# Decay exponents from one 104-row TensorE product per direction, and modulation from unsplit weights in four column strips

## Chip, cores and metric

The kernel runs on one core of one Trainium2 chip. The metric is the device time of one execution in microseconds (us). Before the change, three runs took 2903.76, 2908.97 and 2911.34 us; the median is 2908.97 us.

## What is computed

Two layers of a hybrid diffusion block over 1024 latent tokens and 256 context tokens, width 1024. Each layer modulates a normalised input, projects it, runs attention, a bidirectional state-space scan (SSD) and retention side by side, and projects the mixture back. Two pieces of the reference matter here. The modulation:

```python
shift, scale, gate = jnp.split(jax.nn.silu(c) @ w_ada + b_ada, 3, axis=-1)
shift_c, scale_c, gate_c = jnp.split(jax.nn.silu(c_ctx) @ w_ada + b_ada, 3, axis=-1)
```

and the inner product of the scan, for each direction with its own step sizes (`vc` is `xs * dt`, `cum` the running sum of `dt * -exp(a_log)` in a chunk of 128 tokens):

```python
decay = jnp.exp(jnp.where(lower, cum[:, :, :, None] - cum[:, :, None], -jnp.inf))
scores = jnp.einsum('bcign,bcjgn->bcijg', qc, kc)
y = jnp.einsum('bcijg,bcijgh,bcjghp->bcighp', scores, decay, vc) + ...
```

## The kernel before

Tokens lie in ten tiles of 128. Dense projections run in three TensorE products of high and low parts (`mm3`, L303 with the weights stationary, L305 with the activations stationary): every weight is loaded raw from HBM, rounded into `wh` by ScalarE (L275) and its remainder put into `wl` by GpSimd, or VectorE for some (L277).

A generator of dense work (`dense_all`) is pulled in slices by the scan, attention and retention phases: `SHARE` sets how many microseconds of dense TensorE work each phase may pull, so that the dense products fill TensorE while the other engines do the element work. The framework's scheduler then orders the instructions of each engine from a simulated timeline; on the chip every engine runs its own list in that order. All DMAs are issued from SP's queue, also in order.

*Modulation* (`ada`): `w_ada` is cut into 24 pieces of 256 columns, each 1 MB. Eight (`ADA0`) are needed before the first projection; sixteen (`late`) are spread over layer 0's attention. A piece is split like other weights, then 16 products (L234) with a 4-column stationary operand (high and low parts of two vectors) give a 4 x 256 row, which two small products with `pick` turn into columns (L240).

*The scan* (`pair_phase`) goes over eight pairs of heads; a pair takes five blocks of 256 tokens in layer 0 and four in layer 1, 72 in all. `dt_chunk` makes the step sizes `dt`, the running sums `ncum` and their rows, stored in DRAM (`cumd`, `cume`). For a block, `load_R` fetches a 512 KB broadcast of the rows of `cumd` one block ahead. `pair_stage1` then makes the 128 x 512 matrix `mt` of two heads and two tiles: per head and tile, ScalarE adds the column of `ncum` to the forward row (L740) and scales the forward scores `gf` by `dt` (L743); VectorE adds the backward scores (L746) and takes the minimum with the backward exponent (L749); one exponential (L751) and one product (L752) end it. `pair_stage2`, one block later (`LAG`), multiplies `mt` with the values (L768) and adds the state terms (L775 to L787). PSUM has two buffers `ps_t` (`pst`), which before the change only transposes and small sums use.

```python
te[:, hh, c, :] = R[:, 0, hh, c, :] + ncum            # L740, ScalarE
mt[:, hh, c, :] = gf * dt_f                           # L743, ScalarE
mt = gb * dt_b + mt                                   # L746, VectorE
te = min(R[:, 1, hh, c, :] + ncum_b, te)              # L749, VectorE
te = exp(te); mt = mt * te                            # L751, L752
```

## Time and profile before

| | |
|---|---|
| profiled execution, its own time | 2905.51 us |
| its span | 2903.7 us |
| median of three runs | 2908.97 us |
| TensorE (PE) busy | 2666.6 us, 92% |
| TensorE weight loads (PEld) busy | 2352.1 us, 81% |
| VectorE (DVE) busy | 1925.0 us, 66% |
| ScalarE (ACT) busy | 1211.0 us, 42% |
| GpSimd (POOL) busy | 890.7 us, 31% |
| mean granted TensorE clock | 0.955 |

The busy share of an engine is a mean over stages. TensorE's ends are modelled, so its busy time is no measure of peak; what counts is how long it is idle, and which wait ended last. The granted clock is 1 at 2.4 GHz and 0.5 at 1.2 GHz; a value between says how a stretch is shared by the two.

### The profile page before, as it was taken

How to read it: one execution, taken by the hardware profiler on the slowest of the kernel's cores; microseconds unless marked ns; L12 is line 12 of the kernel's file. 1: busy time of each engine (PE TensorE's matmuls, PEld its weight loads, DVE VectorE, ACT ScalarE, POOL GpSimd, SP SyncE). 2: the span in 40 equal slices, each digit the busy share in tenths (PEclk: the TensorE clock that was granted, in tenths of full speed). 3: DMA queues.
4: the chain of work that ended last, by engine and by line, in shares of the span. 5: the costliest groups of instructions: out<-in, count | busy, mean ns of one | idle time of the engine just before them, and what ended most of it. 6: DMA issues, size and time to landing. Idle time of an engine off the chain costs nothing. (4 is left out here: it accounts for less than half of the span.)

```text
span 2903.7 us, 46416 instructions
## 1 busy us (share of the span) xinstructions
PE 2666.6 (92%) x17164; PEld 2352.1 (81%) x17164; DVE 1925.0 (66%) x4648; ACT 1211.0 (42%) x3226; POOL 890.7 (31%) x766
## 2 busy tenths in 40 slices
PE   6888998899999989998999988997999999999999
PEld 4676877788888789987878767876888888889887
DVE  7668768766677775647446568778667767564751
ACT  5345445435455544423133344444335444442330
POOL 4532322242343421334241323232331112112540
PEclk8898999899999999999999989998999999999999
DMA  7033334321121211114453033333210000101461
GB/s 241 4 110 106 97 93 119 111 66 41 48 69 47 78 29 41 32 53 147 140 183 100 20 91 95 87 106 105 74 41 19 23 15 23 30 24 51 146 212 55
DMA packets 149362, 230.40 MB, mean 79 GB/s; under 512 B 14480, under 2 KB 74128, under 8 KB 149136
## 3 DMA queue, kind: packets, MB, share of 16 engines
q1 hardware_dynamic: 149136, 227.45, 25.3%
q8 instruction: 135, 2.21, 0.3%
q14 instruction: 91, 0.75, 0.1%
HBM read 191.34 MB, written 36.04 MB: 78 GB/s over the span
## 5 line engine op out<-in xcount | busy, mean ns | idle before, releaser
L303 PE MATMUL mm<-ah,wh 128*128 128x512 f32 (+1 forms) x1680 | 635.2, 378 | 34.8 <-DVE zu L357 8.6
L277 POOL TENSOR_TENSOR wl<-raw,wh 128x512 fp32r<-128x512 f32 x288 | 384.3, 1354 | 827.9 <-ACT wh L275 796.0
L303 PE MATMUL mm<-al,wh 128*128 128x512 f32 (+1 forms) x1680 | 626.0, 373 | 1.0 <-DVE al L277 1.0
L303 PE MATMUL mm<-ah,wl 128*128 128x512 f32 (+1 forms) x1680 | 625.9, 373 | 0.0
L305 PE MATMUL mm<-wh,ah 128*128 128x256 f32 x1568 | 456.6, 291 | 9.8 <-DVE zu L357 3.9
L305 PE MATMUL mm<-wl,ah 128*128 128x256 f32 x1568 | 451.2, 288 | 0.4 <-POOL wl L277 0.3
L305 PE MATMUL mm<-wh,al 128*128 128x256 f32 x1568 | 450.0, 287 | 0.0
L303 PEld LDWEIGHTS mm<-ah,wh 128*128 128x128 f32 x1680 | 324.3, 193 | 91.3 <-issue 12.0
L303 PEld LDWEIGHTS mm<-ah,wl 128*128 128x128 f32 x1680 | 324.0, 193 | 51.9 <-issue 1.4
L303 PEld LDWEIGHTS mm<-al,wh 128*128 128x128 f32 x1680 | 324.8, 193 | 50.3 <-DVE al L277 1.4
L950 ACT ACTIVATE e<-s,nb 128x512 f32<-128x512 f32 (+1 forms) x384 | 231.8, 613 | 203.4 <-DVE nb L945 202.5
L305 PEld LDWEIGHTS mm<-wh,ah 128*128 128x128 f32 x1568 | 303.3, 193 | 15.5 <-DVE zu L357 4.2
L305 PEld LDWEIGHTS mm<-wl,ah 128*128 128x128 f32 x1568 | 303.4, 193 | 3.7 <-POOL wl L277 1.0
L305 PEld LDWEIGHTS mm<-wh,al 128*128 128x128 f32 x1568 | 303.1, 193 | 2.7 <-issue 0.5
L940 DVE TENSOR_REDUCE mx<-s 128x1 f32<-128x512 f32 (+1 forms) x400 | 224.0, 588 | 67.0 <-PE s L938 65.7
L275 ACT ACTIVATE wh<-raw 128x512 fp32r<-128x512 f32 x288 | 169.5, 626 | 203.0 <-PE mm L303 81.0
L938 PE MATMUL s<-kT,qT 128*128 128x512 f32 (+1 forms) x800 | 218.0, 376 | 10.9 <-ACT e L950 9.4
L989 PE MATMUL o<-v,aT 128*128 128x128 f32 x1312 | 175.3, 277 | 0.3 <-DVE aT L118 0.3
L706 POOL TENSOR_TENSOR xw<-xn,dtpk 128x512 f32<-128x512 f32 (+2 forms) x96 | 83.2, 877 | 280.7 <-ACT xn L116 63.4
L989 PEld LDWEIGHTS o<-v,aT 128*128 128x128 f32 x1312 | 164.2, 193 | 3.1 <-DVE aT L118 0.5
L938 PEld LDWEIGHTS s<-kT,qT 128*128 128x128 f32 x800 | 134.7, 195 | 31.4 <-ACT e L950 17.7
L749 DVE SCALAR_TENSOR_TENSOR te<-R,dtpk,te 128x128 f32<-128x128 f32 x288 | 131.4, 495 | 13.4 <-ACT te L740 13.3
(266 smaller groups left out, 4837.3 us busy)
## 6 DMA issues: line engine op xcount, KB each, us to landing
raw<-in_wi_dram SPq DMA_DIRECT2D x176, 256.0 KB
R<-cumd SPq DMA_DIRECT2D x72, 512.0 KB
E<-cume SPq DMA_DIRECT2D x144, 128.0 KB
raw<-in_wa_dram SPq DMA_DIRECT2D x64, 256.0 KB
mr<-mix SPq DMA_DIRECT2D x64, 256.0 KB
wr<-in_wa_dram SPq DMA_DIRECT2D x32, 256.0 KB
raw<-in_wo_dram SPq DMA_DIRECT2D x32, 256.0 KB
x<-xr SPq DMA_DIRECT2D x24, 256.0 KB
```

What stands on the lines that cost most here:

```text
L275: nc.scalar.activation(out=hi, in_=x, func=AF.Copy)
L277: e.tensor_tensor(out=lo, in0=x, in1=hi.bitcast(F32), op=ALU.subtract)
L303: nc.tensor.matmul(ps, lhsT=w, rhs=x, start=st, stop=sp)
L305: nc.tensor.matmul(ps, lhsT=x, rhs=w, start=st, stop=sp)
L706: nc.gpsimd.tensor_tensor(out=xw, in0=xn[:, a:a + m].rearrange("p t (h e) -> p t h e", h=2), in1=self.wend[:, a:a + m, h0:h0 + 2].unsqueez ...
L749: nc.vector.scalar_tensor_tensor(out=te[:, hh, c, :], in0=Rv[:, 1, hh, c, :], scalar=col(self.ncum, c, 1, hh), in1=te[:, hh, c, :], op0=AL ...
L938: nc.tensor.matmul(ps[:, 0:n], lhsT=qT[:, 2 * m + s, :], rhs=kT[m][:, t0:t0 + n], start=(s == 0), stop=(s == 1))
L940: nc.vector.tensor_reduce(out=mx[:, ci:ci + 1], in_=ps[:, 0:n], axis=AX.X, op=ALU.max, negate=len(chunks) == 1)
L950: nc.scalar.activation(out=em[:, t0:t0 + n], in_=pss[ci][:, 0:n], func=AF.Exp, bias=nb, accum_out=z[:, 3 * m + ci:3 * m + ci + 1])
L989: nc.tensor.matmul(po[:, 0:P], lhsT=aT[j], rhs=v[:, j, :], start=(j == b0), stop=(j == NT - 1))
```

## The change

Modulation: `w_ada` is read unsplit as six pieces of 512 columns per layer, straight into the `wh` and `wl` buffers. The stationary operand is plain float32, 32 columns wide (two vectors and zeros). Eight products write four column strips of one PSUM bank; `pick`, now 128 x 2, sums the strips.

Scan: `dt_chunk` also forms ln(dt) (a logarithm, and one Newton step through an exponential), adds it to the negated running sum, and stores high and low parts of both rows in DRAM (`crow`). `decay_bufs` fills two buffers with the constant rows of a 104-row product: a mask of -1e30 in 64 rows, ones and selectors. `load_R` then fetches only the rows that vary, in two small DMAs. For each direction one product gives the whole exponent in PSUM, ScalarE takes the exponential in place, and VectorE multiplies with the scores.

```diff
-            for k in range(KT):
-                for j in range(2):
-                    nc.tensor.matmul(ps[0:4, 0:256], lhsT=self.sc[:, k, :], rhs=w[j][:, k, :],
-                                     start=(k == 0 and j == 0), stop=(k == KT - 1 and j == 1))
+            for j in range(2):
+                for g in range(4):
+                    nc.tensor.matmul(ps[32 * g:32 * g + 32, :], lhsT=self.sc[:, 4 * j + g, :], rhs=w[j][:, g, :],
+                                     start=(j == 0), stop=(j == 1))
...
+    def load_a(self, src, j):
+        t = self.w_p.tile([P, 4, 512], F32, tag=("wh", "wl")[j], name=self.nm("wa"))
+        for g in range(0, 4, 2):
+            self.nc.sync.dma_start(out=t[:, g:g + 2, :], in_=src[:, 4 * j + g:4 * j + g + 2, :])
+        return t
...
+        nc.vector.tensor_scalar(out=z, in0=x, scalar1=1e-37, scalar2=None, op0=ALU.max)
+        nc.scalar.activation(out=u, in_=z, func=AF.Ln)
+        nc.scalar.activation(out=z2, in_=u, func=AF.Exp, scale=-1.0)
...
+        r1, r2 = (self.work(x_, (64, 512), F32R) for x_ in ("r1", "r2"))
+        nc.scalar.activation(out=r1[:, 0:tn], in_=pt[0:64, 0:tn], func=AF.Copy)
+        nc.vector.tensor_tensor(out=r2[:, 0:tn], in0=pt[0:64, 0:tn], in1=r1[:, 0:tn], op=ALU.subtract)
...
     def pair_stage1(self, p, bi, last, R):
...
-        for hh, c in hc:
-            nc.scalar.activation(out=te[:, hh, c, :], in_=Rv[:, 0, hh, c, :], func=AF.Identity,
-                                 bias=col(self.ncum, c, 0, hh))
...
-        nc.scalar.activation(out=te, in_=te, func=AF.Exp)
-        nc.vector.tensor_tensor(out=mt, in0=mt, in1=te, op=ALU.mult)
+        for d, G in enumerate(self.grp[p // 4][2]):
+            ps = self.pst()
+            nc.tensor.matmul(ps, lhsT=lt[0:104, d], rhs=rt[0:104, d], start=True, stop=True)
+            nc.scalar.activation(out=ps, in_=ps, func=AF.Exp)
+            f = ps.rearrange("p (h c i) -> p h c i", h=2, c=2)
+            nc.vector.scalar_tensor_tensor(out=f if d else mt, in0=f, scalar=3e38,
+                                           in1=G[:, c0:c0 + 2, :].unsqueeze(1).to_broadcast([P, 2, 2, P]),
+                                           op0=ALU.min, op1=ALU.mult)
+        nc.vector.tensor_tensor(out=mt, in0=mt, in1=f, op=ALU.add)
...
     def load_R(self, p, bi):
-        R = self.unit("R", (P, 2, 2, 256))
...
+        lt, rt = self.lr[0]
+        self.lr.reverse()
+        src = self.crow[bi].rearrange("(a d p) k h t -> a p k d (h t)", a=2, d=2)
+        self.nc.sync.dma_start(out=rt[64:66].bitcast(F32), in_=src[0, p])
+        self.nc.sync.dma_start(out=lt[96:104].bitcast(F32),
+                               in_=self.crow[bi].rearrange("(a d p) k h (c t) -> a p (k h c) d t", a=2, d=2, c=2)[1, p])
```

The scheduler writes each engine's list anew. Three places in these lists follow.

VectorE, one block of the scan (pair 0) before: `te` and `mt` are the block's two tiles, `R` the broadcast rows; the other rows are states, gates and values of other steps.

```order
L749 SCALAR_TENSOR_TENSOR te_1794<-R_1702,dtpk_654,te_1794 128x128 x4
L722 SCALAR_TENSOR_TENSOR st_1727<-st_1727,dtpk_654,s_1730 128x64 x2
L357 SCALAR_TENSOR_TENSOR zu_1764<-zu_1764,mm_1765 128x256
L746 SCALAR_TENSOR_TENSOR mt_1795<-gb_1613,dtpk_654,mt_1795 128x128
L779 SCALAR_TENSOR_TENSOR cv_648<-cv_648,cols_114,o_1851 128x256
L746 SCALAR_TENSOR_TENSOR mt_1795<-gb_1613,dtpk_654,mt_1795 128x128 x3
L357 SCALAR_TENSOR_TENSOR zu_1764<-zu_1764,mm_1904 128x512
L752 TENSOR_TENSOR mt_1795<-mt_1795,te_1794 128x512
```

The same engine and step after the change; `t` is a PSUM buffer of `ps_t`.

```order
L826 SCALAR_TENSOR_TENSOR cv_411<-cv_411,cols_113,o_1549 128x256
L796 SCALAR_TENSOR_TENSOR mt_1512<-t_1513,gf_1430 128x512
L796 SCALAR_TENSOR_TENSOR t_1517<-t_1517,gb_1431 128x512
L799 TENSOR_TENSOR mt_1512<-mt_1512,t_1517 128x512
L796 SCALAR_TENSOR_TENSOR mt_1592<-t_1593,gf_1430 128x512
```

Nine instructions of a block have become three, all with a PSUM operand.

TensorE in the scan of a later pair before: dense rows (L303) around the value product (L768) and the state product (L775).

```order
L303 MATMUL mm_2611<-al_804,wh_2064 128x512
L775 MATMUL s_2455<-cv_647,sf_2241 128x128 x2
L775 MATMUL s_2455<-cv_647,st_1727 128x128 x2
L303 MATMUL mm_2611<-ah_803,wl_2065 128x512
L768 MATMUL o_2411<-mt_2322,xn_1685 64x128 x4
L303 MATMUL mm_2611<-ah_803,wh_2064 128x512
```

After the change, in such a pair (L310 is the dense product, L815 the value product, L822 the state product, L793 the new product, `lr` its operand buffer):

```order
L793 MATMUL t_1887<-lr_1408 128x512
L310 MATMUL mm_2145<-ah_221,wl_1205 128x512
L310 MATMUL mm_2145<-ah_221,wh_1204 128x512
L310 MATMUL mm_2145<-al_222,wh_1204 128x512
L310 MATMUL mm_2145<-ah_221,wl_1205 128x512
L793 MATMUL t_1967<-lr_1428 128x512
L772 MATMUL s_1898<-xw_1896,bn_1286 128x128 x2
L772 MATMUL s_1906<-xw_1904,bn_1286 128x128 x4
L822 MATMUL s_1920<-cv_410,sf_1630 128x128
L822 MATMUL s_1920<-cv_410,st_1525 128x128
L793 MATMUL t_1971<-lr_1428 128x512
L815 MATMUL o_2013<-mt_1882,xn_1493 64x128 x4
```

Products that feed the exponential now stand in TensorE's list, two for a block, and the next block's can stand a few rows behind.

ScalarE in `dt_chunk` after the change (L621 and L622 are the new logarithm and exponential, L485 evacuates a dense product):

```order
L485 ACTIVATE cv_411<-mm_902,cols_113 128x512
L621 ACT_TABLE_LOAD
L621 ACTIVATE dtw_766<-dtw_766 128x128
L485 ACTIVATE cv_412<-mm_967,cols_113 128x512
L622 ACT_TABLE_LOAD
L622 ACTIVATE dtw_766<-dtw_766 128x128
```

Twelve such table loads have been added, two for each of six chunks.

## Rows read from the trace of the kernel before

**Rows 1.** Stages: length; busy PE, PEld, DVE, ACT, POOL; granted clock, DMA share, GB/s.

```profile
180.00:600.00 420.00, 369.78 (x2307) 317.11 (x2308) 330.07 (x933) 202.85 (x527) 127.35 (x95) 0.92 0.35 107
600.00:1500.00 900.00, 847.13 (x5896) 769.47 (x5896) 584.43 (x1290) 380.91 (x1078) 308.55 (x251) 0.97 0.25 75
1650.00:2090.00 440.00, 386.30 (x2312) 331.65 (x2311) 329.69 (x889) 192.74 (x486) 132.97 (x110) 0.92 0.31 93
```

**Rows 2.** Stretches of 10 us in the scan of both layers, columns as above.

```profile
410.00:420.00 10.00, 5.58 (x33) 4.65 (x32) 5.58 (x21) 6.50 (x17) 4.47 (x3) 0.98 0.26 92
...
500.00:510.00 10.00, 5.73 (x43) 4.29 (x41) 9.93 (x31) 4.76 (x13) 1.42 (x1) 0.92 0.63 184
510.00:520.00 10.00, 3.97 (x18) 2.46 (x18) 9.64 (x17) 5.47 (x13) 5.79 (x2) 0.50 0.26 94
...
2000.00:2010.00 10.00, 5.18 (x24) 3.83 (x24) 10.00 (x16) 5.26 (x13) 6.56 (x4) 0.50 0.34 102
```

**Rows 3.** TensorE's waits, from 176 to 600 us, then 1650 to 2090 us: total, times, longest.

```profile
PE t L149 <- DVE cv L505: 19.3, 5, 5.0
...
PE s L712 <- POOL xw L706: 14.8, 5, 4.6
```

**Rows 4.** Groups of instructions by line: busy us, mean ns, idle before and its releaser.

```profile
L749 DVE SCALAR_TENSOR_TENSOR te<-R,dtpk,te 128x128 f32<-128x128 f32 x288 | 131.4, 495 | 13.4 <-ACT te L740 13.3
...
L746 DVE SCALAR_TENSOR_TENSOR mt<-gb,dtpk,mt 128x128 f32<-128x128 f32 x288 | 112.2, 434 | 0.0
...
L740 ACT ACTIVATE te<-R,dtpk 128x128 f32<-128x128 f32 x288 | 91.8, 391 | 61.1 <-DVE cv L505 21.8 <-DMA R<-cumd 16.0 <-PE o L768 13.5
L743 ACT ACTIVATE mt<-gf,dtpk 128x128 f32<-128x128 f32 x288 | 91.4, 390 | 12.5 <-DVE gf L663 5.1 <-DVE cv L505 3.0 <-PE s L775 2.1
...
L752 DVE TENSOR_TENSOR mt<-mt,te 128x512 f32<-128x512 f32 x72 | 56.8, 789 | 1.4 <-ACT te L751 0.7
...
L751 ACT ACTIVATE te<-te 128x512 f32<-128x512 f32 x72 | 45.0, 625 | 43.6 <-DVE te L749 43.4
```

**Rows 5.** Groups with shapes apart: VectorE and ScalarE on 128 x 512 in PSUM.

```profile
L950 ACT ACTIVATE e<-s,nb 128x512 f32<-128x512 f32 x256 | 173.4, 683 | 203.4 <-DVE nb L945 202.5 <-DVE ri L125 0.5
...
L782 DVE TENSOR_TENSOR s<-s,E 128x512 f32<-128x512 f32 x64 | 44.3, 692 | 3.6 <-DMA E<-cume 3.1 <-PE s L775 0.3
```

**Rows 6.** Timeline of the scan: start, length, engine, line; dense products at full clock.

```profile
253.11 0.40 PE L303 MATMUL mm<-ah,wl 128*128 128x512 f32 x1
...
253.34 0.39 PE L303 MATMUL mm<-ah,wh 128*128 128x512 f32 x1
```

**Rows 7.** The start: one 5 us stretch (columns of rows 1), then timeline rows.

```profile
15.00:20.00 5.00, 5.00 (x36) 3.24 (x35) 4.50 (x5) 3.85 (x7) 4.84 (x4) 1.00 0.99 342
...
40.00:45.00 5.00, 3.48 (x21) 1.82 (x19) 4.74 (x14) 1.47 (x6) 3.32 (x2) 0.84 0.59 208
...
12.12 0.38 PE L234 MATMUL mm<-wh,sc 128*4 128x256 f32 x1 [12.12 <-ACT wh L275]
...
52.59 0.69 PE L534 MATMUL mm<-ah,wdt 128*64 128x512 f32 x1
...
59.78 0.50 PE L303 MATMUL mm<-ah,wh 128*128 128x512 f32 x1
```

**Rows 8.** Timeline: modulation products 0.11 us apart, then float32 products, two records each.

```profile
20.10 0.28 PE L234 MATMUL mm<-wl,sc 128*4 128x256 f32 x1
...
20.21 0.28 PE L234 MATMUL mm<-wh,sc 128*4 128x256 f32 x1
...
254.93 1.38 PE L712 MATMUL s<-xw,bn 128*128 128x128 f32 x10
...
267.67 0.66 PE L768 MATMUL o<-mt,xn 128*64 128x128 f32 x8
```

**Rows 9.** The one table load of ScalarE, durations in ns.

```profile
L214 ACT ACT_TABLE_LOAD  x1: 1283/1283/1283, 0.7 to 0.7; - x1
```

**Rows 10.** Weight loads of TensorE that waited for nothing shown: total, times, longest.

```profile
PEld o L768 <- issue: 22.5, 25, 4.4
```

More of the change, by code (lines that the diff above doesn't have):

```diff
@@ L624, in dt_chunk @@
         nc.scalar.activation(out=flat(self.wend), in_=flat(self.wend), func=AF.Exp)
         yield
-        nc.vector.tensor_tensor(out=flat(self.wend), in0=flat(self.wend), in1=flat(self.dt), op=ALU.mult)
+        nc.vector.tensor_tensor(out=flat(self.wend), in0=flat(self.wend), in1=x, op=ALU.mult)
         pt = self.pst()
         for j in range(m):
-            nc.tensor.transpose(pt[0:32, j * P:(j + 1) * P], self.ncum[:, i0 + j, :], self.ident)
-        for nm, func, store in (("cumd", AF.Copy, self.cumd), ("cume", AF.Exp, self.cume)):
-            row = self.work(nm, (32, 512))
-            nc.scalar.activation(out=row[:, 0:tn], in_=pt[0:32, 0:tn], func=func, scale=-1.0)
-            store[c] = self.d_p.tile([8, 2, 2, tn], F32, tag=f"{nm}{l}{c}", name=f"{nm}{l}{c}")
+            nc.tensor.transpose(pt[0:64, j * P:(j + 1) * P], nn[:, j].rearrange("p a h -> p (a h)"), self.ident)
@@ new lines, in dt_chunk @@
+        r1, r2 = (self.work(x_, (64, 512), F32R) for x_ in ("r1", "r2"))
+        nc.scalar.activation(out=r1[:, 0:tn], in_=pt[0:64, 0:tn], func=AF.Copy)
+        nc.vector.tensor_tensor(out=r2[:, 0:tn], in0=pt[0:64, 0:tn], in1=r1[:, 0:tn], op=ALU.subtract)
+        row = self.work("cume", (32, 512))
+        nc.scalar.activation(out=row[:, 0:tn], in_=pt[0:32, 0:tn], func=AF.Exp, scale=-1.0)
+        self.cume[c] = self.d_p.tile([8, 2, 2, tn], F32, tag=f"cume{l}{c}", name=f"cume{l}{c}")
+        for d in range(2):
+            nc.sync.dma_start(out=self.cume[c][:, d], in_=row[16 * d:16 * d + 16, 0:tn])
@@ new lines, in dt_chunk, with decay_bufs @@
+        for b in range(tn // 256):
+            st = self.d_p.tile([32, 2, 2, 256], F32, tag=f"crow{l}{c}{b}", name=f"crow{l}{c}{b}")
+            self.crow[2 * c + b] = st
+            for k, r in enumerate((r1, r2)):
+                nc.sync.dma_start(out=st[:, k], in_=r[:, 256 * b:256 * b + 256].bitcast(F32))
+        yield
+    def decay_bufs(self):
+        nc = self.nc
+        self.lr = []
+        for k in range(2):
+            t = self.unit("lr", (P, TOK), F32R)
+            rt = t[:, 0:1024].rearrange("p (d n) -> p d n", d=2)
+            lt = t[:, 1024:1280].rearrange("p (d n) -> p d n", d=2)
+            self.lr.append((lt, rt))
+            if k:
+                nc.gpsimd.tensor_copy(out=t[0:104], in_=t0[0:104])
+                return
+            t0 = t
+            id64 = self.ident[0:64, 0:64]
+            w = self.work("lrw", (P, 4, 64))
+            nc.vector.memset(t.bitcast(F32)[64:P], 0.0)
+            for d, m in enumerate((self.uf, self.ub)):
+                nc.vector.tensor_tensor(out=w[0:64, d], in0=m[0:64, 0:64], in1=id64, op=ALU.subtract)
+                nc.scalar.activation(out=lt[0:64, d].rearrange("p (q r) -> p q r", r=2),
+                                     in_=w[0:64, d].unsqueeze(2).to_broadcast([64, 64, 2]), func=AF.Copy, scale=-1e30)
+                nc.scalar.activation(out=lt[64:66, d], in_=self.ones[64:66].to_broadcast([2, P]), func=AF.Copy,
+                                     scale=-1.0)
+                for q in range(4):
+                    nc.scalar.activation(out=rt[0:64, d, q * P:(q + 1) * P].rearrange("p (q r) -> p q r", r=2),
+                                         in_=id64.unsqueeze(2).to_broadcast([64, 64, 2]), func=AF.Copy)
+            nc.vector.tensor_tensor(out=w[96:104, 2, 0:4], in0=self.ident[96:104, 96:100],
+                                    in1=self.ident[96:104, 100:104], op=ALU.add)
@@ L1262, in w_order @@
         wi, wa = self.a["wi"], self.a["wa"]
-        q = [(wa[0, i], "gv") for i in ADA0] if l == 0 else []
-        late = iter([(wa[0, i],) for i in range(8, 12)] + [(wa[1, i],) for i in range(12)])
+        q = [(wa[0, i], "ada") for i in ADA0] if l == 0 else []
+        late = iter([(wa[0, i], "ada") for i in (4, 5)] + [(wa[1, i], "ada") for i in range(6)])
         for i in range(N_W):
@@ L1289, in dense_all @@
             yield from xz(5 + j, 3 + j)
-        late = iter([(0, n) for n in range(8, 12)] + [(1, n) for n in range(12)] if l == 0 else [])
+        late = iter([(0, n) for n in (4, 5)] + [(1, n) for n in range(6)] if l == 0 else [])
         def more(i):
@@ L1344, in layer @@
         self.phase(chain(self.dt_rest, self.bc_prep(0, last), self.pair_prep(0),
-                         self.g_prep(0, last)), 26)
+                         self.decay_bufs(), self.g_prep(0, last)), 26)
         share = SHARE[l]
@@ L1393, in run @@
             if j % 2:
-                next(h0)
-                next(h0)
-            if j == 4:
+                for _ in range(4):
+                    next(h0)
+            if j == 2:
                 self.load_dt(0)
```

87 lines of the change are left out of this document (39 added, 48 removed).

## The prediction

> **What bounds the kernel now.** I read the shares of the page first: TensorE is busy for 92% of the span, so at most some 237 us of idle time can be won, and every instruction added to TensorE costs its length wherever TensorE has no gap. Next the busy time by stage, to find the gaps. [rows 1] The two scan stages, 420 and 440 us long, have TensorE busy for 369.8 and 386.3 us: together 50.2 + 53.7 = 104 us of idle time. Their granted clock is 0.92. With 1 for the 2.4 GHz level and 0.5 for the 1.2 GHz level, (1 - 0.92) / 0.5 = 16% of 860 us, 138 us, ran at the low level. The attention stage between them (600 to 1500 us) is 94% busy at 0.97: there TensorE's work is the path.
>
> Then smaller stretches inside a scan, to see who is busy while TensorE is not. [rows 2] At 500 to 520 and 2000 to 2010 us TensorE works for 4.0 to 5.7 of 10 us while VectorE works for 9.6 to 10.0. The first row, at 410 us, is the counterexample: TensorE 5.6 and VectorE also 5.6, a gap at the border of two pairs that no faster VectorE fills. The waits of TensorE say the same. [rows 3] Its longest wait in layer 0 is for a product of VectorE (L505), not of the block itself but queued behind block work; layer 1 has 14.8 us behind GpSimd. So in the scan VectorE is the queue that ends last most often, and TensorE is the engine that pays.
>
> **The change, part by part.** Sums stand against the profiled execution, 2905.5 us; the median of the runs is 3.5 us higher.
>
> *VectorE and ScalarE of a block.* Removed from VectorE are the three groups of 131.4, 112.2 and 56.8 us: 300.4 us, or 4.17 us for each of 72 blocks. [rows 4] Added are three operations on 128 x 512 with a PSUM operand. The nearest row takes 692 ns [rows 5], so 2.08 us a block. VectorE loses 2.09 x 72 = 151 us of the 660 us that it works in the two scan stages, and falls from 77% to 59% of them. ScalarE loses 91.8 + 91.4 + 45.0 = 228 us and gets 144 exponentials in PSUM; by the 683 ns of the one with an accumulator [rows 5] that is 98 us. None of this counts by itself, because neither engine sets the end; it counts through TensorE's gaps.
>
> *TensorE's gaps in the scan.* Of 104 us idle I take 58 us back. Most gaps are of the kind in the last three of rows 2, VectorE saturated; the ones like the first stay. The ends are 20 us (about the 19.3 us that the first of rows 3 shows behind VectorE) and 88 us (85%). With fewer gaps the clock falls less often. Of the 138 us at the low level I take half as matmul time, since the low rows show TensorE 40 to 52% busy [rows 2]; at the full level 69 us become 35, so 35 us is the upper end. I take 25, with 5 as the lower end.
>
> *New products on TensorE.* Two products with 512 columns for each block. Dense products of that width start 0.23 us apart [rows 6], so 144 x 0.23 = 33 us, all on TensorE's list, and all path once the gaps close. A product with 104 rows for 128 takes the same columns; I see no row for less.
>
> Net in the scan: -58 - 25 + 33 = **-50 us**, ends -100 and +8 (-20 - 5 + 33).
>
> *Before the first block.* Twelve table loads of 1.28 us [rows 9] are 15 us of ScalarE. In the four chunks of six that are not a layer's last, dense products cover them, though the evacuations of their PSUM stand behind the loads on ScalarE. The last chunk of a layer gets two loads, a logarithm, an exponential, three VectorE operations and a trip through DRAM before the first block, and `decay_bufs` its fills on ScalarE and one on GpSimd. I take +3 us a layer, **+6 us**; the ends are 0 (the dense work of that phase covers all) and +16 (all table loads exposed).
>
> *Late modulation, layer 0's attention.* Before, a piece of 256 columns is 16 products 0.11 us apart [rows 8], 1.8 us; sixteen pieces are 29 us. After, a piece of 512 columns is 8 float32 products. A float32 product is two records in this trace: the value product stands four times in a row of the list and is eight records [rows 8]. So there are 16 passes of 512 columns. What does a pass take? The eight records of L768 span 0.66 us, one of them 0.27 long, so they start 0.056 us apart at 128 columns; that makes 0.22 us at 512 and 3.6 us a piece if strips run one after another. The full-width records of L712 start (1.38 - 0.28) / 9 = 0.12 us apart, four times that is 0.49 us, 7.8 us a piece: the bad end. If four strips run side by side a piece takes 0.9 us: the good end. I take 2.2 us, between the two that the strip rows allow: 8 x 2.2 = 18 us, **-11 us**; ends -22 and +33. The small `pick` products stay: eight records for a piece twice as wide. The rounding of these weights by ScalarE and GpSimd goes; both are off the path there, so it counts nothing.
>
> TensorE: Matmul & The Clock Gate (Part 3: Packing small matmuls) in the Trainium skill says that small products in different column strips run at once, and gives 2.38x for three strips. By that figure, as an estimate, a piece would take some 1.5 us and this term would be -17 us. The rows of before cannot show it, because no two strips there have a wide moving operand.
>
> *The start.* Layer 0's first four pieces (8 MB) are still loaded, but no split stands between load and product. Before, the first modulation product starts at 12.1, the first projection product at 52.6 and the first dense one at 59.8 us; DMA carries 342 GB/s early and 208 GB/s at 40 us. [rows 7] At 342 GB/s, 8 MB and the 2 MB of `x` take 31 us. Pieces now use the two `wh` and `wl` buffers, so the third waits until the first is multiplied, and the norm still stands after the last. I take **-12 us**, ends -20 and -4.
>
> *Queues.* SP issues two small DMAs where it issued one of 512 KB. Each waits for a product two blocks back to give up its buffer, and behind it stand `E` and raw weights; a block lasts 420 / 40 = 10.5 us, so one block ahead covers it. I cost it at nothing. If that cover is gone, TensorE itself waits at L793, with the dense rows behind it, where before only ScalarE waited (16.0 us on `R` [rows 4]).
>
> Sum: -50 + 6 - 11 - 12 = -67 us: 2838.5 us against the profiled execution, and **2842 us** for the median.
>
> **Rivals.**
>
> *VectorE was the whole cause.* All block gaps close: the scan gives -100 us, and the sum is -117: 2792 us. For it: saturated rows 2. Against: the row at 410 us and GpSimd's 14.8 us. Chance 0.18.
>
> *The strips cost more.* The late pieces take the bad end, +33 instead of -11: 2842 + 44 = 2886 us. For it: weight loads of the 64-column strip product waited 22.5 us in 25 waits that nothing explains [rows 10], 0.9 us each; a piece enters and leaves strips too. TensorEngine Tiling (Key Properties) in the Trainium skill says that changing the tiling mode drains TensorE, which would be such a wait. Against: eight pieces enter and leave only 16 times, 14 us at that price. Chance 0.10.
>
> *The relief does not reach TensorE.* Gaps at pair borders, chains and GpSimd stay; 20 us of gaps and clock come back together while the new products cost 33. The scan is +13 and the sum -4 us: 2905 us, no difference. For it: rows 3 name operations outside the block. Chance 0.09.
>
> *Two PSUM buffers stop TensorE* (slower). A block now holds each `ps_t` buffer from the product over the exponential to VectorE's read, and the next block's product, or a transpose, stands a few rows behind in TensorE's list. If ScalarE or VectorE is late, all dense rows behind wait. The bare chain is 0.23 + 0.68 + 0.69 = 1.6 us, about what stands between two such products in the list. It decides from (67 + 9) / 72 = 1.1 us of added wait a block; at 1.5 us it is 108 us: 2950 us. Against: VectorE at 59% has fewer backlogs of the 5 us kind. Chance 0.11.
>
> **How the numbers follow.** My forecast, 2842 us, has 0.52; its own range is 2805 to 2880. About 0.3%, 9 us, can be told from no change, so faster means below 2900 and slower above 2918. Faster takes the forecast, the first and the second rival: 0.52 + 0.18 + 0.10 = 0.80. The same is 0.09, slower 0.11. The range runs from 2780 (just under the first rival) to 2910 (over the third), and leaves out the slower case and the far good end of the scan and the strips, some 0.18.
>
> **What would show it.** VectorE busy in all near 1925 - 151 = 1774 us, ScalarE down by some 130 us less new fills; L793 at 144 records, 0.23 us apart from the next; TensorE idle in the two scans near 104 - 58 = 46 us with a clock near 0.96; L234 at 192 records, and a late piece in 2 to 3 us; the first dense product near 47 us. Wrong would be: L793 waiting on VectorE or on the DMA of `lr` by more than 1 us a block; idle time in the scans over 80 us; a late piece over 4 us; table loads inside the blocks.

## The result, and the profile after

The changed kernel took 2870.82 us (median of four runs, 2866.96 to 2876.57) against 2906.36 us for the kernel before: a ratio of 0.9878, 95% interval 0.9854 to 0.9902. It is faster by 1.2%, 35.5 us, inside the range and about half of the 67 us forecast. The profiled execution took 2869.1 us, its span is 2867.3 us, 36.4 us less than before, with a mean granted clock of 0.964 for 0.955. All ratios in this document leave out one execution of e8 that took 8641.68 us.

The busy time of the changed kernel, from the page:

```profile
PE 2665.5 (93%) x17116; PEld 2339.0 (82%) x17116; DVE 1781.3 (62%) x4213; ACT 1056.4 (37%) x2678; POOL 772.1 (27%) x688
```

TensorE (PE) is as busy as before within 1.1 us, so all that was won was idle time. VectorE lost 144 us and ScalarE 155 us; neither shows in the time as such. To see where the 36.4 us went I cut both spans at the same events of the program, because the stages moved. Dense products slide over the border between a scan and the step to the first score, and between attention and retention, so those are added up:

| stretch, us | before | after | difference | forecast |
|---|---|---|---|---|
| to the first dense product | 59.8 | 42.0 | -17.8 | -12 |
| to the first value product, layer 0 | 130.9 | 146.0 | +15.1 | +3 |
| scan and step to the first score, layer 0 | 464.9 | 447.2 | -17.7 | -50 for both layers |
| attention, retention, end of layer 0 | 942.6 | 928.1 | -14.5 | -11 |
| layer 1 to its first value product | 116.9 | 121.1 | +4.2 | +3 |
| scan and step to the first score, layer 1 | 419.5 | 400.2 | -19.3 | (above) |
| attention and retention, layer 1 | 649.8 | 663.4 | +13.6 | 0 |
| tail | 119.3 | 119.3 | 0 | 0 |

The busy time by stretch, first the kernel before: the scans of layers 0 and 1, then layer 1's attention and retention. The columns are the stretch, its length, busy time (and instructions) of PE, weight loads, DVE, ACT and POOL, granted clock, DMA share, GB/s.

```profile
190.70:611.10 420.40, 374.97 (x2352) 322.73 (x2353) 330.47 (x917) 199.41 (x518) 132.87 (x98) 0.92 0.36 107
1715.10:2086.60 371.50, 325.57 (x1983) 280.64 (x1982) 287.73 (x780) 165.54 (x423) 113.76 (x91) 0.92 0.33 101
2134.60:2784.40 649.80, 617.91 (x4255) 563.22 (x4254) 434.83 (x1014) 279.24 (x824) 162.38 (x141) 0.98 0.15 47
```

The same three of the changed kernel:

```profile
188.00:576.80 388.80, 373.67 (x2361) 318.41 (x2361) 262.72 (x673) 124.59 (x234) 113.93 (x88) 0.95 0.21 66
1684.40:2036.20 351.80, 335.56 (x2041) 285.96 (x2041) 234.57 (x597) 110.77 (x210) 110.70 (x90) 0.94 0.20 59
2084.60:2748.00 663.40, 620.13 (x4255) 564.25 (x4254) 440.33 (x1014) 279.19 (x824) 160.77 (x141) 0.98 0.15 46
```

Length less busy time is TensorE's idle time: 45.4 + 45.9 = 91 us in the scans before, 15.1 + 16.2 = 31 us after, 60 us back where 58 were forecast. The last row is the surprise: layer 1's attention and retention have the same number of instructions on TensorE, 4255, and take 13.6 us more, 11.4 of them idle, though no line of that code was changed.

What answers to [rows 4] and [rows 5], the operations of a block in the changed kernel. First its groups by line: busy time, mean ns, idle time in front.

```profile
L794 ACT ACTIVATE t<-t 128x512 f32<-128x512 f32 x144 | 82.2, 582 | 146.5 <-PE t L793 142.5 <-DVE v L118 1.4 <-DVE cv L826 1.2
L796 DVE SCALAR_TENSOR_TENSOR t<-t,gb 128x512 f32<-128x512 f32 x72 | 49.9, 694 | 7.6 <-ACT t L794 7.5
L796 DVE SCALAR_TENSOR_TENSOR mt<-t,gf 128x512 f32<-128x512 f32 x72 | 49.5, 687 | 54.8 <-ACT t L794 53.1 <-PE s L772 1.3 <-PE o L815 0.3
L799 DVE TENSOR_TENSOR mt<-mt,t 128x512 f32<-128x512 f32 x72 | 49.2, 683 | 0.4
```

Three operations of 0.68 to 0.69 us, as taken from the 692 ns of [rows 5]; the exponential takes 0.58 us for the 0.68 taken. The new product, with two of the waits in front of it or of its weight load (us, times):

```profile
L793 PE MATMUL t<-lr x144: 389/475/796, 183.8 to 2029.0; 104*128 104x512 f32 x144
...
  DVE mt L796: 19.2, 17
...
  DMA lr<-crow: 3.0, 2
```

All waits of that view add up to some 35 us over 72 blocks, half a microsecond each, where the slower rival decides from 1.1 us; in front of the products themselves 13.6 us are left, 7.4 of them for `mt`. The two small transfers cost 3 us.

### The profile page after: what moved, and what is told of

Same layout as the page of the kernel before. It is cut to its first block, busy times and chain, and to the rows that moved or that the text cites. A ratio compares the mean times of both kernels' runs of the same rounds, so it can differ in the third digit from the quotient of the medians.

```text
span 2867.3 us, 45100 instructions
## 1 busy us (share of the span) xinstructions
PE 2665.5 (93%) x17116; PEld 2339.0 (82%) x17116; DVE 1781.3 (62%) x4213; ACT 1056.4 (37%) x2678; POOL 772.1 (27%) x688
## 4 chain that ended last, share of the span: by engine, by line
PE 76%; DVE 12%; ACT 3%; issue 2%; DMA 2%; POOL 1%; SPq 0%; DVEq 0%; ACTq 0%; POOLq 0%
PE mm L310 34%; PE mm L312 18%; PE t L149 5%; PE o L1037 4%; PE s L986 4%; PE s L772 2%; PE s L822 2%; DVE mx L988 2%; PE o L815 2%; PE t L793 1%; ACT e L998 1%; DVE e L1016 1%; DMA mr<-mix 1%; DVE rs L1156 1%; PE s L1146 1%
## 5 line engine op out<-in xcount | busy, mean ns | idle before, releaser
L310 PE MATMUL mm<-ah,wh 128*128 128x512 f32 (+1 forms) x1680 | 629.4, 375 | 30.1 <-DVE xr L1223 13.8
L310 PE MATMUL mm<-al,wh 128*128 128x512 f32 (+1 forms) x1680 | 622.8, 371 | 1.5 <-DVE al L284 0.9
L310 PE MATMUL mm<-ah,wl 128*128 128x512 f32 (+1 forms) x1680 | 622.4, 371 | 0.6 <-POOL wl L284 0.6
L284 POOL TENSOR_TENSOR wl<-raw,wh 128x512 fp32r<-128x512 f32 x224 | 294.5, 1335 | 769.5 <-ACT wh L282 736.9
L310 PEld LDWEIGHTS mm<-ah,wh 128*128 128x128 f32 x1680 | 322.3, 192 | 85.8 <-issue 13.8
L310 PEld LDWEIGHTS mm<-al,wh 128*128 128x128 f32 x1680 | 322.2, 192 | 51.1 <-issue 1.4
L310 PEld LDWEIGHTS mm<-ah,wl 128*128 128x128 f32 x1680 | 321.2, 191 | 51.2 <-POOL wl L284 1.1
L282 ACT ACTIVATE wh<-raw 128x512 fp32r<-128x512 f32 x224 | 130.0, 625 | 226.2 <-PE mm L310 103.9
L986 PEld LDWEIGHTS s<-kT,qT 128*128 128x128 f32 x800 | 134.3, 193 | 41.3 <-ACT e L998 26.5
L794 ACT ACTIVATE t<-t 128x512 f32<-128x512 f32 x144 | 82.2, 582 | 146.5 <-PE t L793 142.5
```

Source lines behind the costliest of these rows:

```text
L282: nc.scalar.activation(out=hi, in_=x, func=AF.Copy)
L284: e.tensor_tensor(out=lo, in0=x, in1=hi.bitcast(F32), op=ALU.subtract)
L310: nc.tensor.matmul(ps, lhsT=w, rhs=x, start=st, stop=sp)
L794: nc.scalar.activation(out=ps, in_=ps, func=AF.Exp)
L986: nc.tensor.matmul(ps[:, 0:n], lhsT=qT[:, 2 * m + s, :], rhs=kT[m][:, t0:t0 + n], start=(s == 0), stop=(s == 1))
```

## The experiments

Twelve kernels ran. Ratios are against the kernel before, timed on the same chip; the changed kernel itself has 0.9878, and 0.001 is 2.9 us.

| run | ratio | 95% interval |
|---|---|---|
| e1, decay part alone | 0.9930 | 0.9916 to 0.9944 |
| e2, modulation part alone | 0.9892 | 0.9874 to 0.9911 |
| e3, no logarithm on ScalarE | 0.9891 | 0.9874 to 0.9908 |
| e4, one column strip | 0.9972 | 0.9963 to 0.9982 |
| e5, dt steps in twos | 0.9855 | 0.9841 to 0.9870 |
| e6, VectorE work put back | 0.9886 | 0.9870 to 0.9902 |
| e7, products twice | 0.9916 | 0.9898 to 0.9933 |
| e8, three PSUM buffers | 0.9932 | 0.9909 to 0.9954 |
| e9, e5 and another list | 0.9821 | 0.9805 to 0.9837 |
| e10, block in small pieces | 0.9991 | 0.9981 to 1.0000 |
| e11, transfers put back | 0.9924 | 0.9903 to 0.9944 |
| e12, kernel before, another list | 1.0027 | 1.0016 to 1.0039 |

The ratio is of the whole time, and each new list also moves layer 1's attention, which no run here edits (last section of the experiments). So the scans are given by themselves too, from the profiled executions, in us: scans and steps to the first score of both layers, TensorE's idle time in the two scans, and layer 1's attention and retention.

| kernel | scans and steps | idle in the scans | attention and retention, layer 1 |
|---|---|---|---|
| before | 884.4 | 91 | 649.8 |
| changed | 847.4 | 31 | 663.4 |
| e1 | 853.9 | 39 | 648.3 |
| e2 | 880.8 | 81 | 650.0 |
| e6 | 857.5 | 42 | 649.0 |
| e7 | 863.7 | 30 | 651.3 |
| e8 | 873.9 | 50 | 659.3 |
| e10 | 894.6 | 46 | 644.1 |
| e11 | 870.9 | 48 | 646.7 |

e1, e3, e4, e5 and e9 have the scan's code of the changed kernel, and 845.9 to 853.9 us there; so differences up to 7 us say nothing.

### Which part brought the time (e1, e2)

e1 is the kernel before with the new `dt_chunk`, `decay_bufs`, `pair_stage1` and `load_R`; e2 is the rest of the diff. Against the changed kernel:

```diff
 e1
-ADA0 = (0, 2, 1, 3)
+ADA0 = (0, 4, 1, 5, 2, 6, 3, 7)
...
 e2
-            nc.tensor.matmul(ps, lhsT=lt[0:104, d], rhs=rt[0:104, d], start=True, stop=True)
-            nc.scalar.activation(out=ps, in_=ps, func=AF.Exp)
...
+            nc.scalar.activation(out=te[:, hh, c, :], in_=Rv[:, 0, hh, c, :], func=AF.Identity,
+                                 bias=col(self.ncum, c, 0, hh))
...
```

> The decay part alone (new exponent product, exp in PSUM, new dt chain), with the modulation of the kernel before. Theory A (the prelude's own chains of norm and dt swallow an early start, and the decay part earns only in the scans): the two scans together 45 to 55 us shorter than before with TensorE idle there down from 91 to 30 to 40 us, the prelude 4 to 10 us longer, the time 2862 to 2875. Theory B (the new dt steps are what spoils the prelude, +15 us or more there): time 2875 to 2890, and the modulation part alone then keeps its start. Rival C (VectorE was not what held the scans, the gain came with the other part): time above 2895.

> The modulation part alone (unsplit weights in four strips, LATE, first four pieces), with the decay blocks and dt steps of the kernel before. Theory A: first dense product at about 42 us, but chunk 1 stalls as before and the first value product comes at about 183 to 191 us all the same; late pieces earn about 9 us; time 2888 to 2900. Theory B: the first value product at 170 to 176 us, so the head start of 18 us is kept; time 2872 to 2884. If the +10 us of layer 1's attention in the changed kernel comes from this part, attention there is 484 to 488 us here too, else 475 to 478.

Measured, for the stretches of the table above. e1: -0.1, +10.2, -17.0, +3.7, +4.7, -13.5, -1.5, +0.2. e2: -20.7, +6.8, -4.2, -9.6, +0.2, +0.6, +0.2, 0. The medians are 2887.1 us for e1, against 2908.1 us for the kernel before on that chip, and 2876.9 us for e2. Theory B's numbers hold, to within 1 us: the decay part pays 15 us in the two preludes, and the modulation part alone keeps two thirds of its start, with the first value product at 176.8 us. Theory A missed the scans too: e1 earns 30 us there and not 45 to 55, though idle falls to 39 us as it said. The 13.6 us of layer 1's attention come with neither part alone. Alone, the two save 13.3 + 26.7 = 40.0 us in the profiled spans, together 36.4 us.

### Why the early start is given back (e3, e5)

The changed kernel's first dense product comes 17.8 us earlier and its first value product only 2.7 us earlier. Its longest waits of TensorE between the two (us, times, longest):

```profile
PE mm L541 <- DVE edge L492: 9.8, 1, 9.8
PE mm L541 <- ACT ah L456: 7.0, 4, 2.5
```

One stall of 9.8 us, for a PSUM buffer that the evacuation of chunk 0 (`cv` L485 on ScalarE, then `edge` L492 on VectorE) has to free. ScalarE's timeline in that stall (start, length, operation):

```profile
78.97 0.72 ACT L456 ACTIVATE ah<-hu,ada 128x512 fp32r<-128x512 f32 x1 [15.83 <-DVE hu L449]
79.63 0.72 ACT L452 ACTIVATE hu<-hu,ada 128x512 f32<-128x512 f32 x1
80.29 0.72 ACT L456 ACTIVATE ah<-hu,ada 128x512 fp32r<-128x512 f32 x1
80.92 0.61 ACT L282 ACTIVATE ah<-hu 128x512 fp32r<-128x512 f32 x1
81.55 1.28 ACT L621 ACT_TABLE_LOAD   x1
...
83.17 1.28 ACT L634 ACT_TABLE_LOAD   x1
...
84.64 1.44 ACT L485 ACTIVATE cv<-mm,cols 128x512 f32<-128x512 f32 x2
```

ScalarE was idle for 15.8 us and then worked through the norm of chunk 1 and two table loads, with the two evacuations behind them in its list. In the kernel before and in e2 all four evacuations of chunk 0 stand ahead of that norm. Two suspects: the table loads (e3) and the place in the list (e5).

```diff
 e3
-        nc.scalar.activation(out=u, in_=z, func=AF.Ln)
+        nc.vector.tensor_scalar(out=u, in0=z.bitcast(I32), scalar1=math.log(2.0) / 2**23,
+                                scalar2=(0.043 - 127) * math.log(2.0), op0=ALU.mult, op1=ALU.add)
+        nc.scalar.activation(out=z2, in_=u, func=AF.Exp, scale=-1.0)
+        nc.vector.tensor_tensor(out=z2, in0=z, in1=z2, op=ALU.mult)
+        nc.vector.scalar_tensor_tensor(out=u, in0=z2, scalar=-1.0, in1=u, op0=ALU.add, op1=ALU.add)
 e5
-                for _ in range(6):
+                for _ in range(2):
                     next(steps, None)
```

> The changed kernel with ln(dt) from the float's exponent bits on VectorE and two Exp steps instead of one Ln and one Exp: no ACT table load is left in the program's middle, three short VectorE operations and one ACT operation more per chunk, the same values. Theory A (ACT is what the prelude waits for between 78 and 90 us, and the twelve loads of 1.28 us count about half): 4 to 12 us shorter than the changed kernel, all of it before the first value product of each layer. Rival D (GpSimd's polynomial and the norm chain pace the prelude): within 4 us of the changed kernel.

> The changed kernel with the dt steps of a chunk handed out two behind each dense group instead of six, the work unchanged. ScalarE's list then has all four evacuations of chunk 0 ahead of the logarithm and of chunk 1's norm; in the changed kernel two of them stand behind both. Theory A (that place in ScalarE's list is the 9.8 us stall before chunk 1's first product at 80 to 90 us): the wait of L541 for `edge` falls below 3 us, the first value product comes 5 to 12 us earlier, at 176 to 183 us, and the time is 4 to 12 us under the changed kernel. Rival D (the norm chain of chunk 1 would hold that product anyway): the wait only changes its name to `ah` or `al`, the first value product stays within 4 us of 188, the time within 4 us.

In e3 no load is left, and the row reads

```profile
PE mm L541 <- DVE edge L492: 10.2, 1, 10.2
```

with the time unchanged. Twelve table loads cost nothing measurable. In e5 that wait is gone from the list; in its place:

```profile
PE mm L541 <- DVE al L457: 7.1, 3, 2.7
PE mm L541 <- ACT ah L456: 5.6, 3, 2.4
```

The wait changed its name, as rival D has it, and yet the first value product came at 179.0 us, 9 us earlier, as theory A has it: the list's order held back 9 us, and what is left of the early start is held by the norm chain of chunk 1, 12.7 us in these rows. The ratio fell by 0.0023, some 7 us, but the two intervals overlap and the profiled spans differ by 1.7 us; only the earlier value product is clear.

### What the scans were waiting for (e6, e10, e11)

The prediction read the saturated stretches [rows 2] as VectorE's sum of work. Three kernels put back one thing each: work, small operations, transfers.

```diff
 e6, at the end of pair_stage1
+        for _ in range(2):
+            nc.vector.tensor_tensor(out=mt, in0=mt, in1=mt, op=ALU.max)
 e10
-            nc.scalar.activation(out=ps, in_=ps, func=AF.Exp)
+            for h, c in hc:
+                nc.scalar.activation(out=f[:, h, c, :], in_=f[:, h, c, :], func=AF.Exp)
... (the three VectorE operations likewise)
 e11, in load_R
+        R = self.unit("R", (P, 1024))
+        self.nc.sync.dma_start(out=R, in_=self.crow[bi][p].rearrange("k h t -> (k h t)").partition_broadcast(P))
```

> The changed kernel with two more VectorE operations of 128 x 512 in each block that leave `mt` as it is: 72 x 2 x 0.69 = 99 us of VectorE put back of the 151 taken. Theory A (VectorE held the scans, and at the margin each us of it costs TensorE 0.4 us of idle time, as 60 us for 151): TensorE idle in the two scans goes from 31 to 60 to 75 us, the time 30 to 50 us above the changed kernel. Rival F (VectorE has slack now, and the idle time was that of four small operations with their waits on each other): idle below 45 us, time up by 0 to 12 us.

> The changed kernel with each block's two exponentials and three VectorE operations cut into four of 128 columns each, as the kernel before had them: 20 small operations instead of 5, the same values. By the small forms of before (0.32 us on ScalarE, 0.39 to 0.46 us on VectorE) ScalarE gets 60 to 100 us and VectorE 100 to 230 us back. Theory J (many small operations that hand over between engines made the idle time of the scans, not the sum of VectorE's work, since run e6 had VectorE at 80% again with 42 us of idle): idle in the two scans 65 to 95 us, the time 30 to 60 us above the changed kernel. Rival K (the idle time came with the 512 KB transfers and the waits for them): idle below 50 us, the time up by 0 to 20 us.

> The changed kernel with the broadcast of 512 KB for each block put back beside the two small transfers; nothing reads it. Rival K (the transfers made the idle time of the scans): idle in the two scans 55 us or more, the time 15 to 40 us above the changed kernel. Theory J (they did not): idle 25 to 40 us, the time within 8 us of the changed kernel, though the DMA share in the scans goes from 0.2 back to 0.35.

The two scans in e6, e10 and e11, in the columns used above:

```profile
187.90:586.40 398.50, 378.15 (x2397) 321.28 (x2398) 319.63 (x760) 128.25 (x246) 128.28 (x94) 0.97 0.22 68
1693.40:2063.30 369.90, 348.13 (x2108) 295.59 (x2110) 282.78 (x670) 112.60 (x218) 113.94 (x89) 0.94 0.19 57
```

```profile
188.00:608.00 420.00, 395.79 (x2401) 328.50 (x2400) 289.35 (x1029) 158.25 (x474) 120.67 (x93) 0.96 0.20 64
1710.40:2091.60 381.20, 359.75 (x2083) 299.06 (x2082) 257.17 (x888) 136.63 (x403) 109.19 (x89) 0.92 0.18 55
```

```profile
186.60:587.60 401.00, 374.34 (x2360) 317.17 (x2361) 264.97 (x673) 124.13 (x234) 114.47 (x88) 0.95 0.35 114
1702.00:2064.90 362.90, 341.60 (x2042) 288.77 (x2041) 233.94 (x595) 111.04 (x210) 110.00 (x90) 0.93 0.32 101
```

In e6 VectorE is busy for 80% of layer 0's scan, as much as before the change (79%), with 42 us of idle time of TensorE in the two scans for 31, where the kernel before had 91. The scans and steps are 10 us longer, not theory A's 30 to 50. The ratio is within its uncertainty of the changed kernel's, but only because another list gave 14 us back in layer 1's attention and retention. So rival F holds for the scans: VectorE's sum of work was a small part of the cause.

In e10 idle is 46 us, which is rival K's number, but the scans and steps take 47 us more, more than the 37 that the change had won there: 10 of them idle and 37 as busy time of TensorE with the same number of instructions (5241 for 5245). By the ratio it is 33 us, theory J's number, since layer 1's list gave 19 back. Of the 37 us of busy time 25 are in the value products (78.8 us for 53.3): TensorE's list has them in 135 unbroken rows of products, where the changed kernel's has 76. So the small operations hurt in good part through that list, and this run does not show what handing over between engines costs.

In e11 idle is 48 us, below rival K's 55, and the ratio rises by 0.0046, 13 us, below its 15; but the scans and steps take 23.5 us more, which is inside its range, since layer 1's list gave 17 back. ScalarE's waits for that transfer (us, times):

```profile
  ACT zu L363: 9.8, 3
  ACT cv L485: 9.8, 2
  ACT xn L116: 9.2, 2
```

These three tiles come from the pool that gives `R` its buffer. ScalarE waited 28.8 us to write them until a transfer that nothing reads had landed. In the kernel before, ScalarE waited for the transfer only where it reads `R` (L740, 16.0 us [rows 4]). So e11 has at least in part a shortage of buffers that the kernel before did not show, and what the transfers cost there stays open.

None of the three brings back the 91 us of idle time, and no run puts back two at once. One thing that the kernel before had on 648 operations, and the changed block on none, shows when median and longest are read beside the mean. First the block's operations before (shortest/median/longest in ns), then of the changed kernel, then the two operations added in e6:

```profile
L749 DVE SCALAR_TENSOR_TENSOR te<-R,dtpk,te x288: 329/348/2980, 185.2 to 2071.9; 128x128 f32<-128x128 f32 x144
L746 DVE SCALAR_TENSOR_TENSOR mt<-gb,dtpk,mt x288: 333/345/3050, 186.6 to 2074.3; 128x128 f32<-128x128 f32 x144
```

```profile
L796 DVE SCALAR_TENSOR_TENSOR t<-t,gb x72: 686/694/700, 185.6 to 2031.1; 128x512 f32<-128x512 f32 x72
L799 DVE TENSOR_TENSOR mt<-mt,t x72: 673/683/690, 186.8 to 2032.3; 128x512 f32<-128x512 f32 x72
```

```profile
L801 DVE TENSOR_TENSOR mt<-mt x144: 672/683/3044, 186.4 to 2060.4; 128x512 f32<-128x512 f32 x144
```

Here the operations that read only SBUF take up to 3 us; the block's new ones, with an operand in PSUM, never exceed 0.70 us. By mean less median [rows 4], some 26 us of L746 and 42 us of L749 are such stretching. One case in the kernel before, VectorE and then GpSimd (POOL):

```profile
278.70 2.81 DVE L749 SCALAR_TENSOR_TENSOR te<-R,dtpk,te 128x128 f32<-128x128 f32 x1
```

```profile
278.42 2.95 POOL L847 TENSOR_TENSOR cv<-cv,zu 128x1280 f32<-128x1280 f32 x1 [9.77 <-DVE cv L787]
```

The operation of 0.35 us starts 0.28 us behind GpSimd's and ends 0.14 us behind its end. It is no single case: 49 operations of L749 and 33 of L746 took more than 1.5 times the median, all 82 had a GpSimd operation beside them, and each ended 0.15 us behind the end of one. SBUF — State Buffer (SBUF: two separate sides) in the Trainium skill says that a VectorE operation with two SBUF inputs and a GpSimd operation that reads SBUF exclude each other from a shared pair of ports, and that whichever starts first holds it for its whole length. The trace agrees: 2.81 us for 0.35.

How much of TensorE's idle time lies under such operations? Counting every VectorE operation that took over 1.5 times the median of its group and 0.15 us more than it, they cover 15% of the two scans before and 28 of the 91 us of idle time; in the changed kernel 2 of 31 us. So some 25 of the 60 us that were won lay under VectorE operations that were held up. That is an overlap in time: no run kept the old form without GpSimd beside it. In e6 25 of the 144 added operations were stretched too, by some 24 us, so that run put a part of this back together with the work. Where the other 35 us came from is not shown; fewer and larger operations, the transfers, and the backlog behind a stretched operation are all left.

### What TensorE pays (e7, e8)

```diff
 e7
             nc.tensor.matmul(ps, lhsT=lt[0:104, d], rhs=rt[0:104, d], start=True, stop=True)
+            nc.tensor.matmul(ps, lhsT=lt[0:104, d], rhs=rt[0:104, d], start=True, stop=True)
 e8
-            ps = self.pst()
+            ps = self.pss()
```

> The changed kernel with each of the 144 exponent products issued twice into the same PSUM bank: 144 more products of 512 columns, 0.23 us each by the dense ones, 33 us of TensorE. Theory A (TensorE's list is the path in the scans, so the new products cost their whole length): TensorE busy and the time both up by 28 to 36 us. Rival G (the gaps in the scans take them in): the time up by 3 to 15 us, idle in the scans down from 31 to under 15 us.

> The changed kernel with the exponent products in the three PSUM buffers of the score and state products instead of the two that the transposes use. Theory A (the two buffers hardly hold TensorE: waits of L793 for VectorE are some 20 us and half of them would be waits elsewhere): the time within 8 us of the changed kernel, either way. Rival H (the buffers are the remaining limit of the scans): idle there from 31 to under 18 us, the time 10 to 20 us lower. Rival I (the three buffers are needed by states and scores): the time over 10 us higher, with waits of L772 or L822 for VectorE.

The two scans of e7:

```profile
190.30:585.10 394.80, 381.26 (x2419) 322.42 (x2420) 257.08 (x670) 123.87 (x233) 111.87 (x86) 0.98 0.21 63
1705.90:2062.40 356.50, 340.50 (x2101) 286.61 (x2100) 234.59 (x598) 109.97 (x210) 109.66 (x89) 0.98 0.19 58
```

144 more products, 33 us at 0.23 us, make the scans and steps 16 us longer, all of it busy time (826.6 us for 810.4), while idle time in the scans is 30 us for 31. By the ratio they cost 11 us, rival G's price, but another list gave 12 us back in layer 1's attention and retention. The products did not cost their whole length, as theory A has it, and they did not go into the gaps, as rival G has it. The granted clock gave the rest back: it is 0.98 in the scans for 0.95 and 0.94, and of the scans and steps 44 us were at the 1.2 GHz level for 83 in the changed kernel. TensorE had more to do and was at the 2.4 GHz level for more of the scan. e8 comes out with rival I's time, 16 us slower by the ratio and 26.5 in the scans and steps, with idle 50 us, though not with its waits: L772 has 2.7 us in layer 0, the value products wait 5.8 us for `mt` and transposes 7.1 us for `cv`. Two buffers were not the limit.

### What the strips are worth (e4)

```diff
-            for j in range(2):
-                for g in range(4):
-                    nc.tensor.matmul(ps[32 * g:32 * g + 32, :], lhsT=self.sc[:, 4 * j + g, :], rhs=w[j][:, g, :],
-                                     start=(j == 0), stop=(j == 1))
+            for k in range(KT):
+                nc.tensor.matmul(ps[0:32, :], lhsT=self.sc[:, k, :], rhs=w[k // 4][:, k % 4, :],
+                                 start=(k == 0), stop=(k == KT - 1))
```

> The changed kernel with all eight modulation products of a piece on the same 32 columns, one after the other, instead of four strips. Theory A (strips overlap in part: 16 passes start 0.147 us apart in the four strips): here 0.2 to 0.23 us apart, a piece 3.3 to 3.6 us instead of 2.4 to 2.8 us, the twelve pieces 8 to 14 us of TensorE more, the time 4 to 12 us above the changed kernel. Rival E (strips do not overlap, the spacing is the passes' own): the same spacing of 0.147 us and the same time within 3 us.

A whole late piece in four strips in the changed kernel, then one in one strip (start, length), both at a granted clock of 1.00:

```profile
572.54 1.93 PE L234 MATMUL mm<-wa,sc 128*32 128x512 f32 x16
```

```profile
710.25 7.05 PE L233 MATMUL mm<-wa,sc 128*32 128x512 f32 x16
```

In one strip the records start (7.05 - 0.59) / 15 = 0.43 us apart, in four (1.93 - 0.59) / 15 = 0.09 us, so four strips are 7.05 / 1.93 = 3.7 times as fast. One strip costs 27 us by the ratio, where theory A has 4 to 12. Both theories had the spacing wrong. Their 0.147 us are those of one early piece:

```profile
20.94 2.80 PE L234 MATMUL mm<-wa,sc 128*32 128x512 f32 x16
```

That piece ran at a granted clock of 0.66, and the other late pieces that stand in one run of records took 1.92 to 1.93 us like the first row. TensorE: Matmul & The Clock Gate (Part 3: Packing small matmuls) in the Trainium skill gives 2.38x for three strips; with four the rows here show 3.7x. No wait of the 0.9 us that the rival of the strips counted shows at their border: behind the last late piece the next dense product starts at 1039.54 us, 0.5 us after the start of the last strip record, where a record in one strip holds up the next for 0.43 us.

### The list of layer 1's attention (e9, e12)

The changed kernel, e3 and e5 have one and the same list of TensorE from the last value product of layer 1 on; its attention took 485.7, 488.3 and 485.9 us. Other lists gave 470 to 484 us. e9 (on e5) and e12 (on the kernel before) change one number:

```diff
-SHARE = (..., (10, 40, 26, 24, 34, 26, 39, 26, 22, 46, 46, 59, 45, 78, 26))
+SHARE = (..., (10, 40, 26, 24, 34, 26, 39, 26, 20, 46, 46, 59, 45, 78, 26))
```

> The kernel with the dt steps in twos (run e5), and one number of layer 1's table SHARE changed from 22 to 20, so that the work is the same and the scheduler writes another list for layer 1's attention. That attention took 485.7, 488.3 and 485.9 us in three kernels that share one list of TensorE there, and 474 to 478 us in five kernels with other lists. Theory L (the 10 us are the list's, with transposes put a little ahead of VectorE's sums): attention in layer 1 takes 474 to 481 us here, waits of L149 for `nb` and `e` fall from 8 us to under 4 us, the time 2856 to 2863. Rival M (the faster scans bring attention into a state that costs the 10 us whatever the list): 483 to 489 us again, the time within 4 us of run e5.

> The kernel before, with nothing but the one number of layer 1's table SHARE changed from 22 to 20, as in run e9. Theory L (the order that the scheduler writes for layer 1's attention is worth some 10 us either way, in any kernel): that attention and the retention behind it, 649.8 us before, move by 5 to 15 us up or down, the time by as much. Rival N (20 is simply the better number, so the gain of run e9 says nothing of the changed kernel's list): attention and retention 5 to 12 us shorter, the time 5 to 12 us lower. Rival O (the list is worth little, and run e9's gain came from elsewhere): within 3 us.

The waits of TensorE there, in the changed kernel and in e9:

```profile
PE t L149 <- DVE e L1016: 4.1, 3, 1.8
PE t L149 <- DVE nb L993: 3.9, 3, 2.4
```

```profile
PE t L149 <- DVE e L1016: 2.6, 3, 1.8
PE t L149 <- DVE nb L993: 2.4, 2, 2.1
```

In e9 the attention takes 481.7 us, just over theory L's 481, with 34 instructions of TensorE more in it, and from the last value product to the end of retention 700.9 us for 709.4 in e5 and 711.8 in the changed kernel; the waits fall from 8.0 to 5.0 us, not under 4. The time is 2855.7 us, the best of all, and its ratio lies below e5's with no overlap of the intervals. In e12 the same number lengthens attention and retention by 12.2 us (662.0 for 649.8) and the time by 0.27%, 8 us. So 20 is not the better number; the list is worth some 10 us either way, in either kernel. The three kernels with the one list have 661 to 666 us for attention and retention; the changed kernels of e6, e7, e10 and e11, each with another list, have 644 to 651.

## Why the prediction was right, and where its size came from

- **Gaps in the scan** (-58): right in size, 91 to 31 us, but in part by luck, since its reason was half right. VectorE held TensorE, but not by its sum of work: with VectorE at 80% again (e6) only 11 us of idle time came back. Some 25 us lay under operations of VectorE that GpSimd held up, which the prediction counted as work (the 495 ns of L749 for a median of 348); the rest is open.
- **New products** (+33): 33 us of work at the dense rows' 0.23 us; e7 shows that the next 33 us cost 16 in the scans and steps, the clock giving back the rest.
- **Clock** (-25): the step that failed in the scan. In scans and steps to the first score TensorE is busy for 810.4 us, 18 more than before; 33 less 18 leaves about 15 us for the clock. It rose to 0.95 and 0.94, not 0.96: 83 us of scans and steps are still at the low level, for 131 before. The term also asked for more than its own sign: 25 of at most 35 us need 71% of the low time gone, and 0.96 for 0.92 is half of it. With the gaps this makes the scan -37 us for -50.
- **Before the first block** (+6): +15 us in e1, at the upper end. The reason given for that end, table loads, is wrong (e3). What cost it is the order: the new dt steps let two evacuations slip behind the next chunk's norm in ScalarE's list (e5), so that early dense products were stopped for 9.8 us.
- **The start** (-12): 17.8 us, near the good end. The loads ran as estimated, 338 GB/s over these 42 us for 342; the time set behind them was too long. But I counted a start that everything behind it would follow. The next chain, chunk 1's norm, did not: start and preludes together are +1.5 us for -6.
- **Late modulation** (-11): -14.5 us in the stretch behind the scan. A late piece takes 1.93 us for 2.2 taken, so eight of them take 15 us where the sum had 18. Of the two prices that the prediction had for a piece in one strip, 3.6 and 7.8 us, e4 shows 7.05, near the one called the bad end; 2.2 came out near only because four strips divide it by 3.7. That is luck too.
- **Queues** (0): right; 3 us of waits for `lr`.
- **Not in the sum at all**: +13.6 us in layer 1's attention and retention, from a list that the scheduler wrote anew though no code there changed. This is the largest single part of the 31 us between forecast and result, with 13 us from the scan and 7.5 from start and preludes; the late pieces brought 3.5 back.

Of the rivals, "VectorE was the whole cause" fell with e6, "the strips cost more" with e4 and the rows of the pieces, "two PSUM buffers" with half a microsecond of wait a block and e8. "The relief does not reach TensorE" held in a part: the two preludes and the list of layer 1's attention cost 33 us. One sum in the prediction is wrong without changing the forecast: the good end of the scan is -88 - 35 + 33 = -90 us, not -100, so the first rival would be 2802 us and not 2792.

The best version is e9: all of the change, dt steps in twos and another list, 0.9821 of the time before.

## What to carry to other kernels

Read shortest, median and longest of an operation, not only the mean: a tail of 3 us on operations of 0.35 us was here a wait for another engine that no list of waits shows. An earlier start is worth only what the next chain in order lets through, so look at what stands in front of the evacuations in each engine's list, on the first chunk above all. Where a scheduler writes the lists, any change rewrites stages that it does not touch; before 10 us are put down to a cause, move one number that changes no work and see how far the time moves. Compare the stretch that was edited too: here the total hid 12 to 19 us of what e6, e7, e10 and e11 cost.

## What the runs showed of the hardware

- Adding 144 products of 0.23 us to the scans raised their granted clock from 0.94 and 0.95 to 0.98, and made the scans and steps 16 us longer in place of 33.
- A float32 product with 32 columns of weights and 512 moving columns takes two records 0.43 us apart in one strip; interleaved over four strips, sixteen of them take 1.93 us for 7.05, both at a granted clock of 1.00.
- The block's VectorE operations with an operand in PSUM have no tail (longest 0.70 us); those that read only SBUF were stretched to 3 us beside GpSimd, and all 82 stretched ones of L749 and L746 ended 0.15 us behind a GpSimd operation.
